# Other step counts for convolution and pooling chains in a hybrid pooling and convolution block

## The chip, the cores and the metric

The kernel runs on one core of one Trainium2 chip. The metric is the device time in microseconds (us), the median of several runs. The engines are TensorE (PE, with its weight loads as PEld), VectorE (DVE), ScalarE (ACT), GpSimd (POOL) and SyncE (SP), which issues most of the DMAs.

## The reference

One layer (DEPTH 1), 2048 frames, model width 1024, float32. What is computed:

```python
h = rmsnorm(x, norm_mix_pre[l])
proj = h @ w_in[l]
u_pool, u_glu, g_a, g_b = jnp.split(proj, [512, 1536, 2560], axis=-1)
branch_a = pool_mixer(u_pool, pool_w[l], pool_scale[l], w_pool_out[l])
branch_b = conformer_conv(u_glu, conv_w[l], conv_b[l], conv_ln_g[l], conv_ln_b[l], w_conv_out[l])
merged = jax.nn.sigmoid(g_a) * branch_a + jax.nn.sigmoid(g_b) * branch_b
x = x + rmsnorm(merged @ w_o[l], norm_mix_post[l])
h = rmsnorm(x, norm_mlp_pre[l])
f = jnp.square(jax.nn.relu(h @ w_up[l])) @ w_down[l]
x = x + rmsnorm(f, norm_mlp_post[l])
```

`pool_mixer` takes trailing means over 2, 4, 8 and 16 frames minus the frame itself, a linear map for each of the 4 groups of 128 channels, a scale and a projection. `conformer_conv` is a gated unit, a causal depthwise convolution of 31 taps over 512 channels, a LayerNorm, a swish and a projection.

## The kernel before, in words

The frames are worked on in two blocks of 1024 (`b` 0 and 1). Channels lie on the 128 partitions, frames along the free axis. The large matrix products use a scheme of seven products instead of eight for two-by-two blocks; such a group of seven is an `Octet` (products 1, 2, 6, 5, 7, 3, 4 in this order, the first two octets of a run mixed by `START`). Each operand is a high and a low part of reduced precision, made by `split` and `split_w` (ScalarE rounds the high part at L195 or L202, VectorE subtracts at L119). So one product is 24 matmuls of 128x128 by 128x512 (L240). The low parts of the weights (`wl`) are computed for block 0, stored in `kept`, and loaded again for block 1.

The order of the main line is: for block 0 the octets `glu` (two), `pool` (one), `ga` (two), `gb` (two), then the product `A` (the pooling branch, `branch_a`, eight tiles); for block 1 `pool`, `glu`, `ga`, `gb`; then block 0's `B` (`merge`, eight tiles) and `wo` (`out_proj`, eight tiles of two products each), block 1's `A`, block 0's `up` (eight octets), block 1's `B`, `wo` and `up`, and `down` for both blocks. Products are counted here from 0 in this order: ga begins at 21, gb at 35, A at 49, block 1's pool at 57, its ga at 78, its gb at 92, B at 106, wo at 114, A at 130, up at 138.

Beside the main line run the chains of the change. `conv_steps` does the convolution on VectorE, 31 taps for each of four channel groups, one step a tap (L756 for the first, L760 for the others); the group's sum is added (`sm`), and the row stored to DRAM (`yd`). `pool_steps` does the window sums (L116, L869), a split, six matmuls on TensorE (`mix`), an evacuation (L881 on ScalarE, L882 on VectorE) and a store to `mxd`, from where `A` loads it. `norm_steps` is the LayerNorm: matmuls L790 and L791 for the mean, subtractions of the mean from rows loaded again, L438 for the sum of squares, the root (small instructions of L461 to L493), L505 to spread it over the partitions, then scale, swish and a store to `zd`, from where `B` loads it.

A chain is a Python generator in a `Lane`. After each product, `bg()` calls each lane, which adds its `rate` to a credit and takes so many steps; a step that yields a number ends the turn and skips products. The instructions of these steps are put behind the product's mark (`behind`), and a scheduler then orders each engine by priority. `tc.high_priority(offset=...)` moves instructions forward in this order. On the chip each engine works in its order, SP's queue of DMAs too, so what stands behind a waiting instruction waits as well. The `tr` tiles (nine buffers), `wl` (three), `wr` (four) and the PSUM tiles for products (three) are shared by main line and chains; the accumulator `y` of the convolution has one buffer.

`tail` is the lane of block 0's convolution and pooling; what is left of it goes on in block 1 as the lane at L1202, behind which the norm of block 0 follows. `pooling()` (L1204) adds, after block 1's `pool` octet, a lane for its pooling and one for its convolution, `conv1`, which waits for the other two. `conv1` goes on in B (rate 0.5), `wo` (the rate of L1223) and `up` (1.2, then 2.8), with block 1's norm behind it.

Of the kernel before, what the change touches and what calls it, by code (L numbers as in the profile page):

```python
# [65 lines left out]
def block_kernel(  # L66
# [132 lines left out]
    def split_w(src, n=TB, low=None):  # L199
        hi = mk(p_wh, "wh", F32R)  # L200
        lo = mk(p_wl, "wl", F32R)
        nc.scalar.copy(hi[:, :n], src[:, :n])  # L202
        if low is None:
            sub(lo[:, :n], src[:, :n], f32(hi[:, :n]))
        else:
            load(f32(lo), low)
        return hi, lo
# [3 lines left out]
    def load_w(src, key):  # L211
        with tc.high_priority(offset=ahead[0]):
            raw = mk(p_wr, "wr")
            load(raw, src)
            known = kept.get((key, "low"))
            w = split_w(raw, low=known)
        if known is None:
            kept[key, "low"] = dram("kept")
            later.append((kept[key, "low"], f32(w[1])))
        return w  # L220

    kept, later, due = {}, [], []
# [45 lines left out]
    def weight_parts(src, key, b, keep, raw):  # L268


        s = {}

        def get(q):
            if q not in raw:
                raw[q] = mk(p_wr, "wr")
                load(raw[q], src[q])
            return raw[q]

        def minus(a, b, op=sub):
            o = mk(p_ws, "ws")  # L280
            op(o, a, b)
            return o

        def source(i):
            if i in (1, 2, 4):
                return get({1: 0, 2: 1, 4: 3}[i])
            if (key, i, "sum") in kept and b:
                if ("s", i) not in raw:
                    raw["s", i] = mk(p_wr, "wr")
                    load(raw["s", i], kept[key, i, "sum"])  # L290
                return raw["s", i]
            if i == 7:
                return minus(get(0), get(2))
            if i in (5, 6) and 1 not in s:
                s[1] = minus(get(2), get(3), add)
            if i == 6:
                s[2] = minus(s[1], get(0))
                return s[2]
            if i == 5:
                return s[1]  # L300
            return minus(get(1), s[2])

        def save(i, what, tile):
            kept[key, i, what] = dram("kept")
            later.append((kept[key, i, what], f32(tile)))

        def part(i):
            with tc.high_priority(offset=ahead[0]):
                for q in {1: (0,), 2: (1,), 4: (3,), 7: (0, 2), 5: (2, 3), 6: (2, 3, 0), 3: (1,)}[i]:
                    if (key, i, "sum") not in kept or not b:  # L310
                        get(q)
                if (key, i, "sum") in kept and b:
                    source(i)
            with tc.high_priority(offset=40):
                t = source(i)
                w = split_w(t, low=kept[key, i, "low"] if keep and b else None)
            if keep and not b:
                save(i, "low", w[1])
                if keep == "sums" and i not in (1, 2, 4):
                    save(i, "sum", t)  # L320
            return w

        return part
# [451 lines left out]
    def norm_steps(b, lag):  # L775

        sh, sl = split(sums[b], *TR)
        yield 3
        mu = mk(p_ss, "r", F32, (P, W))[:, :TB]
        y = {}  # L780

        def prefetch(c):
            y[c] = tr()
            load(y[c], yd[b, c, 0])

        prefetch(0)
        for t in (0, 1):
            s = slice(t * T, (t + 1) * T)
            rb = mk(ps_rb, "rb", F32, (P, T))
            nc.tensor.matmul(rb, ones, sh[:, s], start=True, stop=False)  # L790
            nc.tensor.matmul(rb, ones, sl[:, s], start=False, stop=True)  # L791
            nc.scalar.activation(mu[:, s], rb, AF.Copy, scale=1.0 / CW)
        yield 1
        ss = mk(p_ss, "sm")
        for c in range(CC):
            if c + 1 < CC:
                prefetch(c + 1)
            sub(y[c], y[c], mu)
            load(yd[b, c, 0], y[c])
            sq = ss if c == 0 else tr()  # L800
            nc.scalar.activation(sq, y[c], AF.Square)
            if c % 2:
                yield 1
            if c:
                add(ss, ss, sq)
        yield lag
        r = mk(p_ss, "r", F32, (P, W))[:, :TB]
        halves = [ss[:, t * T : (t + 1) * T] for t in (0, 1)]

        def got(t, rb):  # L810
            nc.scalar.copy(r[:, t * T : (t + 1) * T], rb)

        yield from inv_rms_steps(halves, inv_c, TR, lag, got)
        prefetch(0)
        yield 1
        sg, hl = {}, {}
        for c in range(CC + 2):
            if c < CC:
                if c + 1 < CC:
                    prefetch(c + 1)  # L820
                mul(y[c], y[c], r)
                sg[c] = tr()
                nc.scalar.activation(
                    sg[c], y[c], AF.Sigmoid, scale=col(C_LG + c), bias=col(C_LB + c)
                )
                nc.scalar.activation(
                    y[c], y[c], AF.Identity, scale=col(C_LG + c), bias=col(C_LB + c)
                )
            if 0 < c <= CC:
                mul(y[c - 1], y[c - 1], sg[c - 1])  # L830
                hl[c - 1] = split(y[c - 1], *TR)
            if c > 1:
                for i, part in enumerate(hl[c - 2]):
                    load(zd[b, c - 2, i], f32(part))
            yield 1
# [9 lines left out]
    def pool_steps(b, alone):  # L845

        def get(g):
            s, u = window(W), tr()
            load(s, ud[g][:, b * TB : b * TB + W])
            load(u, ud[g][:, HALO + b * TB : HALO + b * TB + TB])  # L850
            return s, u

        s, u = get(0)
        yield 1
        for g in range(CC):
            w, m = WINDOWS[g], 1
            while m < w:
                lo = HALO - (w - 2 * m)
                s2 = window(W) if alone or m in (2, 8) else mk(p_ss, "r", F32, (P, W))
                add(s2[:, lo:], s[:, lo:], s[:, lo - m : W - m])  # L860
                s, m = s2, 2 * m
                yield
            if b == 0:
                mul(
                    s[:, HALO : HALO + w],
                    s[:, HALO : HALO + w],
                    cst[:, C_CNT + g * HALO : C_CNT + g * HALO + w],
                )
            nc.vector.scalar_tensor_tensor(  # L869
                u, s[:, HALO:], 1.0 / w, u, op0=ALU.mult, op1=ALU.subtract  # L870
            )
            hl = split(u, *TR)
            if g + 1 < CC:
                s, u = get(g + 1)
            yield 3
            ps = psum("mix")
            for t in (0, 1):
                h = slice(t * T, (t + 1) * T)
                matmuls(ps[:, h], pw, g, [tuple(p[:, h] for p in hl)], main=False)
            hi, lo = tr(F32R), tr(F32R)  # L880
            nc.scalar.activation(hi, ps, AF.Copy, scale=col(C_PSC + g))  # L881
            nc.vector.scalar_tensor_tensor(  # L882
                lo, ps, col(C_PSC + g), f32(hi), op0=ALU.mult, op1=ALU.subtract
            )
            yield
            load(mxd[b, g, 0], f32(hi))
            load(mxd[b, g, 1], f32(lo))
            yield
# [238 lines left out]
    lanes = []  # L1127
# [25 lines left out]
    tail = Lane(1.9, conv_steps(0, (0,)))  # L1153
# [18 lines left out]
    def more():  # L1172
        pool_weight()
        tail.gens.append(chain_of(pool_steps(0, True), conv_steps(0, (1, 2, 3), False)))
        tail.rate = 2.2

    pi = pool_in(0, parts)[0]
    run(
# [6 lines left out]
    rest = tail.gens  # L1185
# [6 lines left out]
    def marked(gen, k):  # L1192
        yield from gen
        done.add(k)
# [4 lines left out]
        yield from gen  # L1199

    rest = [marked(chain_of(*rest), "conv")]
    lanes += [Lane(3.8, *rest, marked(norm_steps(0, 1), "norm"))]  # L1202

    def pooling():  # L1204
        lanes.append(Lane(2, marked(pool_steps(1, False), "pool")))
        lanes.append(Lane(2.0, behind_all(conv_steps(1, (0, 1, 2, 3)), "conv", "pool")))


# [8 lines left out]
    conv1 = lanes.pop()  # L1217
# [2 lines left out]
    lanes.append(conv1)  # L1220
    merged = merge(0, bg)
    fetched = []
    conv1.rate = 2  # L1223
    parts = Parts(lambda ops: token_parts(ops, lambda c, t: parts.raw(c, t), *BIG, TR))
    chain = out_proj(
        0, merged, ((0,), (1,)), bg, parts.some, lambda: fetched.extend(fetch_spread(mxd, 1))
# [301 lines left out]
    for n, (s, i, b) in enumerate(jobs):  # L1528
# [8 lines left out]
        if s == LAST or b == 0:  # L1537
            w = [part(i, o) for o in (0, 1)]
# [80 lines left out]
```

## Time and profile before

| | |
|---|---|
| median of 3 runs | 2405.51 us (2405.14 to 2408.62) |
| profiled execution | 2413.18 us, its span 2411.4 us |
| mean granted TensorE clock in it | 0.965 |
| TensorE matmul, busy | 2234.3 us, 93% of the span |
| weight load, busy | 1824.6 us, 76% |
| VectorE, busy | 1688.1 us, 70% |
| ScalarE, busy | 1036.1 us, 43% |
| DMA | 566.98 MB, mean 235 GB/s |

The profile is one execution, taken by the hardware profiler. A line of a profile names the source line, the engine, the operation and the tiles as output<-inputs. In brackets at the end of an instruction stands how long the engine was idle before it and what ended that. Busy matmuls overlap, so the pace of TensorE is read from their number in a stretch (x714 in 160 us) and not from the busy time. A row of stages gives the stretch in us from the span's start, its length, busy time and count for PE, PEld, DVE, ACT and POOL, the granted clock as a share, the DMA engines' share and GB/s.

### The profile page before, as it was taken

Reading aid. Unit: us, or ns where it says so; the run is one execution under the profiler, and the core shown is the slowest. Engines: PE = TensorE matmul, PEld = TensorE weight load, DVE = VectorE, ACT = ScalarE, POOL = GpSimd, SP = SyncE. Lnnn points to the kernel's source line nnn. Section 1 sums busy time; section 2 is a strip of 40 time slices with the busy share of each in tenths; the row PEclk is TensorE's granted clock in tenths of the full one; section 3 lists DMA queues with packets and bytes.
Section 4 is the critical chain, followed back from the end, with each engine's and each line's share of the span. In section 5 each row is a group of like instructions: output and inputs, shape, how many; then the busy total and the mean of one; then the engine's idle time right before and its main releaser. Section 6 shows DMA issues by size and latency. Waiting matters only on the chain.

```text
span 2411.4 us, 25045 instructions
## 1 busy us (share of the span) xinstructions
PE 2234.3 (93%) x9600; PEld 1824.6 (76%) x9600; DVE 1688.1 (70%) x1672; ACT 1036.1 (43%) x1077; POOL 1.0 (0%) x10
## 2 busy tenths in 40 slices
PE   6999988897989989999989988999999999999984
PEld 5788877686778877787868866888788887788763
DVE  5897757897668549898644496777644656696776
ACT  5434442333532425444543564555544322223542
POOL 0000000000000000000000000000000000000000
PEclk9999999998999989999999989999999999999996
DMA  4678997676897774335496655687755445447873
GB/s 169 245 263 294 345 349 250 231 246 232 293 352 283 254 290 158 131 128 181 160 360 251 221 198 210 229 301 261 296 203 192 164 162 201 178 148 250 291 285 156
DMA packets 158951, 566.98 MB, mean 235 GB/s; under 512 B 18672, under 2 KB 18800, under 8 KB 158832
## 3 DMA queue, kind: packets, MB, share of 16 engines
q1 hardware_dynamic: 146448, 520.30, 59.9%
q10 hardware_dynamic: 12384, 45.09, 4.8%
q8 instruction: 75, 1.23, 0.2%
q14 instruction: 44, 0.36, 0.0%
HBM read 378.06 MB, written 187.27 MB: 234 GB/s over the span
## 4 chain that ended last, share of the span: by engine, by line
PE 72%; DVE 15%; DMA 6%; issue 4%; ACT 3%; SPq 0%; DVEq 0%; ACTq 0%
PE down L240 23%; PE up L240 17%; PE wo L240 7%; PE gb L240 5%; DVE y L760 4%; PE ga L240 4%; PE B L240 4%; PE glu L240 4%; PE A L240 4%; PE pool L240 3%; DVE tr L119 2%; DVE tr L116 2%; DMA tr<-yd 2%; DMA wr<-w_in 1%; DVE wl L119 1%
## 5 line engine op out<-in xcount | busy, mean ns | idle before, releaser
L240 PE MATMUL up<-big,wh 128*128 128x512 f32 x1792 | 493.7, 397 | 42.7 <-ACT tr L390 21.4
L240 PEld LDWEIGHTS up<-big,wh 128*128 128x128 f32 x1792 | 341.8, 192 | 121.9 <-ACT tr L390 24.0
L202 ACT CAST wh<-wr 128x1024 fp32r<-128x1024 f32 x176 | 185.0, 1051 | 467.4 <-issue 80.5
L240 PE MATMUL down<-tr,wh 128*128 128x512 f32 x896 | 353.6, 395 | 13.0 <-DVE tr L119 13.0
L240 PE MATMUL down<-fo,wh 128*128 128x512 f32 x896 | 352.9, 394 | 9.6 <-ACT fo L1383 9.5
L760 DVE SCALAR_TENSOR_TENSOR y<-v,cst,y 128x1024 f32<-128x1024 f32 x240 | 307.1, 1280 | 3.2
L240 PE MATMUL up<-big,wl 128*128 128x512 f32 x896 | 280.8, 395 | 0.0
L240 PE MATMUL down<-fo,wl 128*128 128x512 f32 x896 | 278.9, 393 | 0.0
L202 ACT CAST wh<-ws 128x1024 fp32r<-128x1024 f32 x124 | 130.3, 1052 | 257.9 <-PE up L240 97.0
L240 PEld LDWEIGHTS down<-tr,wh 128*128 128x128 f32 x896 | 170.0, 190 | 53.1 <-DVE tr L119 18.0
L240 PEld LDWEIGHTS down<-fo,wh 128*128 128x128 f32 x896 | 170.2, 190 | 48.6 <-ACT fo L1383 13.3
L240 PEld LDWEIGHTS up<-big,wl 128*128 128x128 f32 x896 | 171.6, 192 | 36.3
L240 PEld LDWEIGHTS down<-fo,wl 128*128 128x128 f32 x896 | 170.0, 190 | 35.3
L1383 ACT CAST fo<-tr 128x1024 fp32r<-128x1024 f32 x102 | 107.0, 1050 | 188.0 <-DMA tr<-fd 128.3
L116 DVE TENSOR_TENSOR big<-big,down 128x1024 f32<-128x1024 f32 x88 | 106.9, 1218 | 110.4 <-PE down L240 105.9
L119 DVE TENSOR_TENSOR wl<-ws,wh 128x1024 fp32r<-128x1024 f32 x116 | 141.5, 1220 | 58.3 <-ACT wh L202 57.9
L119 DVE TENSOR_TENSOR tr<-tr,fo 128x1024 fp32r<-128x1024 f32 x102 | 124.6, 1221 | 72.9 <-ACT fo L1383 72.7
L119 DVE TENSOR_TENSOR wl<-wr,wh 128x1024 fp32r<-128x1024 f32 x103 | 125.5, 1218 | 46.5 <-ACT wh L202 45.9
L240 PE MATMUL glu<-big,wh 128*128 128x512 f32 x448 | 127.3, 405 | 21.5 <-DVE big L119 9.2
L240 PE MATMUL ga<-big,wh 128*128 128x512 f32 x448 | 123.3, 398 | 6.2 <-DVE tr L116 5.9
L240 PE MATMUL wo<-big,wh 128*128 128x512 f32 x512 | 127.1, 390 | 0.2 <-DVE big L119 0.2
L116 DVE TENSOR_TENSOR tr<-tr,tr 128x1024 f32<-128x1024 f32 x65 | 79.4, 1221 | 66.6 <-ACT tr L536 57.9
(151 smaller groups left out, 3147.9 us busy)
## 6 DMA issues: line engine op xcount, KB each, us to landing
tr<-fd SPq DMA_DIRECT2D x116, 512.0 KB, 5.3
wl<-kept SPq DMA_DIRECT2D x81, 512.0 KB, 4.0
wr<-w_up SPq DMA_DIRECT2D x68, 512.0 KB, 4.3
wr<-w_down SPq DMA_DIRECT2D x66, 512.0 KB, 4.3
kept<-wl SPq DMA_DIRECT2D x65, 512.0 KB, 5.3
fd<-tr ACTq DMA_DIRECT2D x54, 512.0 KB, 3.5
wr<-w_in SPq DMA_DIRECT2D x53, 512.0 KB, 5.6
fd<-tr SPq DMA_DIRECT2D x50, 512.0 KB, 3.5
```

The lines of the kernel that those rows point to most:

```text
L116: return nc.vector.tensor_tensor(o, a, b, op=ALU.add)
L119: return nc.vector.tensor_tensor(o, a, b, op=ALU.subtract)
L202: nc.scalar.copy(hi[:, :n], src[:, :n])
L240: i = nc.tensor.matmul(ps, w[wp][:, (at + k) * P : (at + k + 1) * P], rhs[k][xp], start=start and n == 0, stop=stop and n == len(order) - ...
L760: nc.vector.scalar_tensor_tensor(acc, v[:, k : k + TB], wk, acc, op0=ALU.mult, op1=ALU.add)
L1383: nc.scalar.copy(hi, t)
```

## The change

Four rates change, and two scopes of priority are written in another way.

```diff
@@ load_w
-            w = split_w(raw, low=known)
+            w = split_w(raw) if known is None else None
+        if w is None:
+            with tc.high_priority(offset=260):
+                w = split_w(raw, low=known)
@@ weight_parts, part
-                w = split_w(t, low=kept[key, i, "low"] if keep and b else None)
+                if not (keep and b):
+                    w = split_w(t)
+            if keep and b:
+                with tc.high_priority(offset=40):
+                    w = split_w(t, low=kept[key, i, "low"])
@@ more
-        tail.rate = 2.2
+        tail.rate = 3
@@ 
-    lanes += [Lane(3.8, *rest, marked(norm_steps(0, 1), "norm"))]
+    lanes += [Lane(3.2, *rest, marked(norm_steps(0, 1), "norm"))]
@@ pooling
-        lanes.append(Lane(2, marked(pool_steps(1, False), "pool")))
+        lanes.append(Lane(1.7, marked(pool_steps(1, False), "pool")))
@@ 
     merged = merge(0, bg)
     fetched = []
-    conv1.rate = 2
+    conv1.rate = 6
```

The number of instructions is the same; their order differs. In the two orders the convolution taps stand in these stretches of VectorE:

| stretch of VectorE's order | taps before | taps after |
|---|---|---|
| up to the end of block 0's pool octet | 15 | 15 |
| block 0's ga and gb, first two reads of A | 16 | 34 |
| from there to the read of block 1's 30th product | 93 | 75 |
| the rest of block 1's ga and gb, B | 36 | 31 |
| from B's last read to the first read of block 1's A (wo) | 17 | 47 |
| block 0's up | 71 | 46 |

| on TensorE, the place ahead of product | before | after |
|---|---|---|
| block 0's four mixes | 32, 37, 42, 48 | 30, 34, 38, 43 |
| block 1's four mixes | 72, 77, 82, 88 | 73, 78, 84, 91 |
| first matmul of block 0's norm (L790) | 87 | 87 |
| first matmul of block 1's norm (L790) | 174 | 165 |

## The prediction

> **What bounds the kernel now.** I began with the busy times of the page, then the stages cut at the borders of the matrix products, and last the waits inside the stages that lose time.
>
> ```profile
> PE 2234.3 (93%) x9600; PEld 1824.6 (76%) x9600; DVE 1688.1 (70%) x1672; ACT 1036.1 (43%) x1077; POOL 1.0 (0%) x10
> ...
> 160.00:320.00 160.00, 160.00 (x714) 132.43 (x713) 124.25 (x138) 69.04 (x70) 0.00 (x0) 1.00 0.84 310
> ...
> 386.00:590.00 204.00, 178.72 (x736) 143.50 (x736) 180.28 (x151) 65.50 (x65) 0.00 (x0) 0.93 0.68 237
> 590.00:720.00 130.00, 117.67 (x484) 96.25 (x485) 80.07 (x84) 57.95 (x60) 0.00 (x0) 0.93 0.85 306
> ...
> 852.00:912.00 60.00, 52.91 (x205) 42.14 (x204) 32.33 (x42) 15.36 (x19) 0.00 (x0) 0.86 0.78 290
> ...
> 1004.00:1116.00 112.00, 112.00 (x496) 92.72 (x494) 111.41 (x96) 51.38 (x50) 0.00 (x0) 1.00 0.33 124
> ...
> 1204.00:1249.00 45.00, 35.74 (x148) 29.10 (x147) 23.45 (x21) 25.43 (x25) 0.00 (x0) 0.89 0.95 349
> ```
>
> A row gives the length of a stage, then busy time and instruction count for PE, PEld, DVE and ACT, then the granted clock. In a stretch without a gap TensorE does 714 matmuls in 160 us, 4.46 per us, so one product of 24 matmuls takes 5.4 us. At that pace 386:590 needs 736 / 4.46 = 165 us and took 204: 39 us are lost. The same sum gives 21.5 us lost in 590:720, 14 in 852:912 and 12 in 1204:1249. From 1004 to 1116 VectorE is busy all the time and TensorE still loses nothing: a full VectorE is no loss as long as nobody waits for it. The change touches only chains on VectorE, so its worth is read from the stages where TensorE waits for them.
>
> ```profile
> PE rb L790 <- ACT tr L195: 12.3, 1, 12.3
> PE pool L240 <- DMA wl<-kept: 5.4, 1, 5.4
> PE glu L240 <- DVE tr L116: 5.4, 1, 5.4
> ```
>
> These are TensorE's longest waits in 386:590. The first is the mean of the convolution: its operand is split on ScalarE, after the last convolution tap of block 0. Two of the three hang on the depth of VectorE's queue, the one in the middle is a load of weights.
>
> **The change, part by part.** The two rewritten priority scopes cost nothing: with them alone, the build has the same instructions, buffers and waits in the same order on every engine. What is left is four rates. The counts below are those of the two orders, as tabled above.
>
> *Rate 2.2 to 3: block 0's gates and the start of A.* Pooling must be done before the product A.
>
> ```profile
> 320.00:340.00 20.00, 13.90 (x51) 10.65 (x50) 4.87 (x4) 5.11 (x6) 0.00 (x0) 0.83 0.97 373
> ...
> 323.51 1.29 DVE tr L882
> ...
> 324.82 5.25 DMA mxd<-tr
> ...
> 330.12 5.75 DMA big<-mxd
> ...
> 334.68 0.80 PE L240 MATMUL A<-big,wh 128*128 128x512 f32 x1 [5.66 <-DMA big<-mxd]
> ...
> 336.93 2.76 PE L240 MATMUL A<-big,wh 128*128 128x512 f32 x6
> ...
> 340.98 1.52 PE L240 MATMUL A<-big,wh 128*128 128x512 f32 x6
> ```
>
> The last pooling result is made, stored and loaded again in 12.3 us (323.51 to 335.87) while TensorE stands. In the slice 320:340 it does 51 matmuls, worth 11.4 us: 8.6 us lost. The last mix moves from ahead of product 48 to ahead of product 43, five products or 27 us earlier, so the 12.3 us are covered: gain 8.6, nothing else of that load being late. The row also shows that a stop costs more than its idle time: six matmuls take 2.76 us right behind it and 1.52 us later. The Trainium skill, "TensorE: Matmul & The Clock Gate", Part 1, says that an idle window of about 3.4 us halves the clock until a busy window has passed; the trace agrees (2.76 against 1.52 us). By that rule the stop would cost its 5.66 us and half a window, 7.4; the sum takes the slice's 8.6.
>
> The price: 18 convolution taps move into this stage and the first two A products.
>
> ```profile
> L760 DVE SCALAR_TENSOR_TENSOR y<-v,cst,y 128x1024 f32<-128x1024 f32 x240 | 307.1, 1280 | 3.2
> ...
> L119 DVE TENSOR_TENSOR wl<-ws,wh 128x1024 fp32r<-128x1024 f32 x116 | 141.5, 1220 | 58.3 <-ACT wh L202 57.9
> ...
> 290.00:320.00 30.00, 30.00 (x134) 24.79 (x133) 16.46 (x16) 11.72 (x13) 0.00 (x0) 1.00 0.98 355
> ```
>
> 18 x 1.28 = 23 us of VectorE. In 160:320 it has 160 - 124 = 36 us to spare, 13.5 of them after 290, where most taps go, and pooling work of about six instructions leaves that place. Behind the taps on VectorE stand the low halves of weights (wl) and the gates' sums; whoever is late there stops TensorE. I take 3 us of loss, between 0 (the spare time holds all) and 8 (a third of the 23 us shows).
>
> *Rates 3.8 to 3.2 and 2 to 1.7: block 1's pool, glu and ga.* Up to the 30th product of block 1, where norm and pooling meet, VectorE has 75 taps instead of 93 and three pooling instructions fewer: 18 x 1.28 + 3 x 1.22 = 26.7 us less, from 180.3 to 153.6 us. TensorE needs 165. So VectorE stops being the longer side. If its own idle time stays (204 - 180 = 24 us), the stage takes 154 + 24 = 178 us; TensorE alone, with the load of weights kept (5.4 us and a slow clock behind), about 173 (5.4 x 8.6 / 5.66 = 8). The gain is at most 27; at least some 8, if the 12.3 us of L790 shrink to a third and all other waits stay, since they come from the order of the queue. I take 20: the sum for VectorE gives 26, and I leave 6 to waits that the order makes. L790 stands ahead of product 87 in both orders, and I expect it to lose most of its 12.3 us.
>
> *The rest of block 1's gates.* Pooling ends later (mix ahead of product 91, before 88), beside the norm steps.
>
> ```profile
> 603.11 1.23 DVE L119 TENSOR_TENSOR tr<-tr,r 128x1024 f32<-128x1024 f32 x1 [8.22 <-DMA tr<-yd]
> ...
> 620.52 2.93 PE L240 MATMUL ga<-big,wh 128*128 128x512 f32 x6 [5.88 <-DVE tr L116]
> ```
>
> VectorE waits 8.22 us for a stored convolution row to come back, and the gate's sum behind it holds TensorE for 5.88 us. The loads stand among the same neighbours in both orders, so this stays. Five taps fewer lie behind it, but pooling's tiles now share the nine `tr` buffers with the norm. I take a gain of 2, between -6 (that wait once more) and +6 (it is gone).
>
> *Rate 2 to 6: the output projection.* From its first tile to the first read of A, VectorE has 47 taps instead of 17: 30 x 1.28 = 38.4 us more.
>
> ```profile
> 763.00:798.00 35.00, 35.00 (x156) 29.00 (x155) 34.02 (x29) 14.17 (x17) 0.00 (x0) 1.00 0.57 180
> 798.00:858.00 60.00, 57.63 (x251) 46.69 (x250) 23.78 (x34) 30.60 (x39) 0.00 (x0) 0.98 0.79 280
> 858.00:879.00 21.00, 17.31 (x63) 13.62 (x62) 0.34 (x2) 1.05 (x1) 0.00 (x0) 0.82 0.72 274
> ...
> 797.75 1.23 DVE L116 TENSOR_TENSOR tr<-tr,tr 128x1024 f32<-128x1024 f32 x1
> 808.63 1.23 DVE L116 TENSOR_TENSOR tr<-tr,tr 128x1024 f32<-128x1024 f32 x1 [9.65 <-ACT tr L536]
> 809.89 0.69 DVE L116 TENSOR_TENSOR tr<-tr 128x512 f32<-128x512 f32 x1
> 818.51 0.16 DVE L461 TENSOR_SCALAR sa<-rb 128x4 f32<-128x4 f32 x1 [7.93 <-PE rb L438]
> ...
> 878.75 1.22 DVE L122 TENSOR_TENSOR tr<-A,tr 128x1024 f32<-128x1024 f32 x1 [20.66 <-DMA tr<-sad]
> ```
>
> VectorE's first 35 us are full and keep nearly the same taps (17; 18 of the 47 now); the others fall into 798:858, with 36 us free, and before 878.75, where it waits 20.66 us for a gate. Laid out one after the other: the square sum of 797.75 ends about 2.5 us later (a tap, a convolution's sum), 801.5; 8 taps bring it to 812; the sums of 808.63 and 809.89 with a tap between them end at 815, not 810.6; 4 taps and a sum later, at 821.5, the root begins that began at 818.51. Its input, the sum, is taken by TensorE's L438, which VectorE waited 7.93 us for, so 4.4 us later is early enough. 14 taps among the adds behind it (18 us) fill waits there and end the stretch some 8 us later than now, near 866, still ahead of 878.75. ScalarE's gains (L571) wait for some of these adds, with reads of PSUM behind them. I take 2 us of loss, between 0 and 18 (all 14 taps among the adds show). The loss in 852:912 has another cause, the loads of A, and stays.
>
> *The end of block 0's up products.* With 46 taps left instead of 71, the second norm starts ahead of product 165, not 174, and is over before the last two octets, which have extra stores.
>
> ```profile
> PE up L240 <- ACT tr L390: 9.3, 1, 9.3
> ...
> 1203.11 3.73 SPq L125 DMA_DIRECT2D fd<-tr  x3
> 1206.93 0.44 SPq L125 DMA_DIRECT2D tr<-yd  x1
> ...
> 1213.32 1.22 DVE L122 TENSOR_TENSOR tr<-tr,r 128x1024 f32<-128x1024 f32 x1 [3.30 <-DMA tr<-yd]
> ```
>
> The norm's last load stands behind those stores on SP's queue; VectorE waits for it, ScalarE for VectorE, TensorE for ScalarE: 9.3 us, 12 with the slow clock. I take 9.5 gained, between 2 (the norm meets a like stop earlier) and 12. That the taps of 1004:1116 go gains nothing: TensorE lost nothing there.
>
> **The sum**: 8.6 - 3 + 20 + 2 - 2 + 9.5 = 35.1 us. The profiled execution took 2413.2 us (span 2411.4 and 1.8 around it), so it would take 2378. It was 7.7 us above the median of the runs, 2405.5; 35.1 off that is 2370.4.
>
> **The rivals.** *Order, not depth*: the waits of 386:590 come from where the instructions stand and not from how many there are. For it: the three longest waits there make 23 of the 39 us, one of them is a load of weights, and the rest are short pieces. Against: VectorE was busy 88% of that stage. Then 3 of the 20 us are won, 18 in all: 2387. *All of it*: each gain at its upper bound and no loss, 8.6 + 27 + 6 + 12 = 53.6: 2352.
>
> *The projection pays* (slower): six taps a tile hold VectorE's adds back, ScalarE's gains wait for them ahead of its reads of PSUM, and TensorE stops in each tile of the second half. The price is 38.4 us of taps, and 1.52 times that where the clock falls (8.6 us lost for 5.66 of waiting at A's start): 58 us, against the 2 in the sum: 2370 + 56 = 2426. It decides once over 37 us show, that is, if hardly any of the 58 us that VectorE stands idle from 763 to 879 can be used. For it: in-order adds with ScalarE behind. Against: its longest idle times end at TensorE and a load, not at its own work.
>
> *Nothing moves*: all of it is shifted within the slack. The Trainium skill, "Perfetto Trace Analysis", Identifying the Most-Contended Engine, says to improve the engine with the highest occupancy; here that is TensorE (93%) and the change takes no work from it, so by that rule alone the time stays 2405.5. The trace speaks against it: 5.66 us of waiting for pooling at A and 12.3 at L790 are idle TensorE. That the rates do nothing at all is excluded by the orders.
>
> **How the numbers follow.** Forecast 0.62, order 0.18, all of it 0.07, the projection 0.10, nothing moves 0.03. About 0.2%, 5 us, is what a measurement of this kernel can tell from no change. Faster is 0.62 + 0.18 + 0.07 = 0.87, of which 0.01 may end within 5 us: 0.86; same 0.04; slower 0.10. The bounds of the terms reach from 54 us won to 13 lost if all fall together; the forecast's own range is 2354 to 2388. With the order rival and the full gain inside, and the projection left out, the range is 2348 to 2400.
>
> **What would show it.** Right: no wait on mxd at the first A product of block 0; L790 below 4 us; VectorE under 95% of a stage from pool to ga that is some 20 us shorter; no stop near the end of the first up, and a norm over before it; roots in the projection less than 5 us later against their product. Wrong: new waits of TensorE for wl or for L505 in the projection, a mix that waits beside the norm, or waits as long as before in block 1's glu with fewer taps in front of them.

## The result and the profile after

The kernel with the change took 2364.76 us in the median of 4 runs (2361.49 to 2370.55). The kernel before, on the same chip, took 2405.32 us (2402.55 to 2408.62, 4 runs). The ratio is 0.9833, with a 95% interval of 0.981 to 0.9857: 1.7% or some 41 us faster. In a second set of runs (**e0_again**) it took 2370.28 us beside 2411.61, a ratio of 0.9827 [0.9805, 0.9848]. The profiled execution took 2370.55 us, its span is 2368.8 us against 2411.4 before.

The first fence holds the page's busy times, the next one the stages, cut where a product's first matmul runs: block 0's ga and gb (164:325), its A (325:368), then block 1's pool and glu, ga and gb, block 0's B and `wo`, block 1's A, and block 0's `up`. The change shifts all lines of the file after its first edits by 3 to 7: L240, L390, L438, L505, L760 and L790 are now L243, L397, L445, L512, L767 and L797.

```profile
PE 2223.5 (94%) x9600; PEld 1818.9 (77%) x9600; DVE 1690.4 (71%) x1672; ACT 1037.7 (44%) x1077; POOL 1.0 (0%) x10
```

```profile
164.00:244.00 80.00, 80.00 (x358) 66.17 (x357) 70.83 (x77) 35.76 (x36) 0.00 (x0) 1.00 0.80 290
244.00:325.00 81.00, 81.00 (x362) 67.03 (x361) 68.56 (x75) 34.57 (x36) 0.00 (x0) 1.00 0.94 344
325.00:368.00 43.00, 43.00 (x192) 35.60 (x190) 31.76 (x27) 20.80 (x27) 0.00 (x0) 1.00 1.00 380
368.00:511.00 143.00, 127.32 (x518) 102.04 (x517) 115.23 (x97) 48.83 (x49) 0.00 (x0) 0.93 0.70 239
511.00:603.00 92.00, 87.03 (x371) 70.87 (x370) 71.11 (x77) 37.81 (x39) 0.00 (x0) 0.94 0.80 279
603.00:688.00 85.00, 80.00 (x340) 65.16 (x340) 55.40 (x47) 42.40 (x42) 0.00 (x0) 0.96 0.95 350
688.00:735.00 47.00, 44.13 (x196) 36.21 (x195) 35.10 (x30) 12.51 (x13) 0.00 (x0) 1.00 0.92 339
735.00:824.00 89.00, 89.00 (x398) 73.76 (x397) 80.81 (x83) 38.99 (x48) 0.00 (x0) 1.00 0.72 244
824.00:884.00 60.00, 51.67 (x202) 41.41 (x201) 44.01 (x52) 17.13 (x22) 0.00 (x0) 0.86 0.80 303
884.00:1204.00 320.00, 311.81 (x1370) 256.95 (x1369) 243.42 (x224) 172.97 (x172) 0.00 (x0) 0.99 0.49 178
```

VectorE and ScalarE are busy as long as before, to 2.3 us. Of the 42.6 us that the span lost, 31.8 were idle time of TensorE; the other 10.8 us are a lower busy time for the same 9600 matmuls. A of block 0 and the projection (735:824) run without a gap, the projection with VectorE at 80.8 of 89 us. Block 1's pool to ga still loses, at a granted clock of 0.93, with VectorE at 79% (115.23 + 71.11 of 235 us). Block 1's A (824:884) loses as much as before.

TensorE's waits that answer to those of the prediction, in the whole of the span:

```profile
PE pool L243 <- DMA wl<-kept: 7.4, 1, 7.4
...
PE up L243 <- ACT tr L397: 6.9, 3, 4.7
...
PE gb L243 <- DMA wl<-kept: 5.0, 2, 4.2
PE A L243 <- DMA tr<-mxd: 4.4, 2, 2.3
PE ga L243 <- ACT tr L736: 4.2, 1, 4.2
```

The norm's mean (L790, 12.3 us) is no longer among them, and the waits of `up` for L390 (now L397) are shorter: the 9.3 us one is gone, and the 4.7 left is in block 1's `up`. Two smaller ones, inside B of block 0 and A of block 1:

```profile
PE B L243 <- DMA big<-zd: 2.9, 1, 2.9
```

```profile
PE A L243 <- DVE tr L122: 3.9, 1, 3.9
```

The table compares stages of the profiled executions, each from the first matmul of a product to the first of the next, in us. "Again" is e0_again; the other columns are the experiments below. The prediction drew one border in another place: its stage "pool, glu and ga" ends ahead of product 87, inside ga.

| stage | before | changed | again | e1 | e2 | e3 | e4 | e6 | e7 | e8 | e9 | e10 | e12 | e13 |
|---|---|---|---|---|---|---|---|---|---|---|---|---|---|---|
| ga and gb, block 0 | 161.0 | 161.0 | 161.0 | 161.0 | 161.0 | 161.0 | 161.0 | 161.0 | 161.0 | 161.0 | 161.0 | 161.0 | 161.0 | 161.7 |
| A, block 0 | 52.2 | 43.5 | 43.5 | 44.9 | 52.2 | 53.0 | 53.7 | 43.5 | 53.4 | 43.5 | 43.5 | 43.5 | 43.5 | 43.5 |
| pool, glu, block 1 | 145.4 | 142.9 | 143.8 | 149.2 | 143.6 | 148.0 | 144.7 | 146.3 | 144.2 | 136.2 | 143.3 | 140.8 | 147.1 | 145.9 |
| ga, block 1 | 107.8 | 91.7 | 93.0 | 94.4 | 80.6 | 107.0 | 94.5 | 95.3 | 80.0 | 84.5 | 90.1 | 90.3 | 108.0 | 108.2 |
| gb, block 1 | 87.3 | 85.2 | 84.1 | 85.1 | 92.8 | 88.2 | 87.0 | 85.6 | 94.6 | 85.9 | 83.8 | 84.5 | 76.2 | 76.2 |
| B, block 0 | 43.5 | 46.7 | 48.9 | 43.5 | 54.6 | 43.5 | 43.5 | 43.5 | 54.0 | 45.0 | 45.1 | 44.8 | 43.5 | 43.5 |
| wo, block 0 | 88.5 | 88.5 | 88.5 | 88.5 | 88.5 | 88.5 | 88.5 | 88.5 | 88.5 | 88.5 | 88.5 | 88.5 | 88.5 | 88.5 |
| A, block 1 | 59.8 | 60.5 | 61.8 | 55.6 | 58.5 | 52.3 | 54.4 | 53.1 | 59.8 | 59.2 | 61.7 | 51.0 | 53.1 | 52.3 |
| up, block 0 | 337.1 | 320.0 | 319.8 | 339.4 | 333.3 | 319.8 | 340.2 | 319.6 | 319.8 | 320.2 | 331.5 | 320.1 | 320.1 | 321.4 |
| B, block 1 | 43.5 | 43.5 | 43.5 | 43.5 | 59.5 | 43.5 | 43.5 | 43.5 | 43.5 | 43.5 | 43.5 | 43.5 | 43.5 | 43.5 |

From before to changed: A -8.7, pool and glu -2.5, ga -16.1, gb -2.1, B +3.2, A of block 1 +0.7, `up` -17.1. That is -42.6 us, the difference of the two spans. What stands ahead of and behind these stages cancels: the start is 1.9 us earlier, the `up` of block 1 3.8 us shorter, and the rest (`down`) 5.8 us longer (691.3 against 685.5).

### The profile page after: what moved, and what is told of

Read it like the earlier page. It is cut to its first block, busy times and chain, and to the rows that moved or that the text cites. A ratio compares the mean times of both kernels' runs of the same rounds, so it can differ in the third digit from the quotient of the medians.

```text
span 2368.8 us, 25052 instructions
## 1 busy us (share of the span) xinstructions
PE 2223.5 (94%) x9600; PEld 1818.9 (77%) x9600; DVE 1690.4 (71%) x1672; ACT 1037.7 (44%) x1077; POOL 1.0 (0%) x10
## 4 chain that ended last, share of the span: by engine, by line
PE 79%; DVE 10%; DMA 6%; issue 2%; ACT 2%; SPq 0%; DVEq 0%; ACTq 0%
PE down L243 24%; PE up L243 23%; PE wo L243 7%; PE ga L243 5%; PE gb L243 5%; PE glu L243 4%; PE A L243 4%; PE B L243 4%; PE pool L243 2%; DVE tr L119 2%; DMA tr<-fd 1%; DVE tr L116 1%; DVE y L767 1%; DVE big L116 1%; DMA wr<-w_in 1%
## 5 line engine op out<-in xcount | busy, mean ns | idle before, releaser
L243 PE MATMUL up<-big,wh 128*128 128x512 f32 x1792 | 489.9, 395 | 28.5 <-ACT big L195 10.3
L243 PEld LDWEIGHTS up<-big,wh 128*128 128x128 f32 x1792 | 339.7, 190 | 105.8 <-ACT big L195 12.4
L243 PE MATMUL down<-tr,wh 128*128 128x512 f32 x896 | 354.9, 396 | 12.2 <-DVE tr L119 12.2
L243 PE MATMUL down<-fo,wh 128*128 128x512 f32 x896 | 354.1, 395 | 11.9 <-ACT fo L1390 11.9
L767 DVE SCALAR_TENSOR_TENSOR y<-v,cst,y 128x1024 f32<-128x1024 f32 x240 | 307.6, 1282 | 3.6
L243 PE MATMUL down<-fo,wl 128*128 128x512 f32 x896 | 280.6, 395 | 0.0
L243 PE MATMUL up<-big,wl 128*128 128x512 f32 x896 | 279.2, 393 | 0.0
L243 PEld LDWEIGHTS down<-tr,wh 128*128 128x128 f32 x896 | 170.8, 191 | 53.3 <-DVE tr L119 17.9
L243 PEld LDWEIGHTS down<-fo,wh 128*128 128x128 f32 x896 | 171.0, 191 | 50.3 <-ACT fo L1390 14.6
L243 PEld LDWEIGHTS down<-fo,wl 128*128 128x128 f32 x896 | 171.4, 191 | 35.7
L243 PEld LDWEIGHTS up<-big,wl 128*128 128x128 f32 x896 | 170.4, 190 | 35.8
L1390 ACT CAST fo<-tr 128x1024 fp32r<-128x1024 f32 x102 | 107.0, 1050 | 188.0 <-DMA tr<-fd 120.2
L119 DVE TENSOR_TENSOR wl<-wr,wh 128x1024 fp32r<-128x1024 f32 x103 | 125.6, 1220 | 43.5 <-ACT wh L202 41.0
L243 PE MATMUL glu<-big,wh 128*128 128x512 f32 x448 | 125.2, 399 | 18.8 <-DVE big L119 10.0
L243 PE MATMUL wo<-big,wh 128*128 128x512 f32 x512 | 127.1, 390 | 0.2 <-DVE big L119 0.2
L243 PE MATMUL ga<-big,wh 128*128 128x512 f32 x448 | 123.0, 397 | 4.2 <-ACT tr L736 4.2
L243 PE MATMUL gb<-big,wh 128*128 128x512 f32 x448 | 121.6, 394 | 0.0
```

The lines of the kernel that those rows point to most:

```text
L119: return nc.vector.tensor_tensor(o, a, b, op=ALU.subtract)
L243: i = nc.tensor.matmul(ps, w[wp][:, (at + k) * P : (at + k + 1) * P], rhs[k][xp], start=start and n == 0, stop=stop and n == len(order) - ...
L767: nc.vector.scalar_tensor_tensor(acc, v[:, k : k + TB], wk, acc, op0=ALU.mult, op1=ALU.add)
L1390: nc.scalar.copy(hi, t)
```

## Experiments

> The changed kernel itself once more, so that the next ones can be compared with it on the same chip: 2365 us, 40 below before.

That was 2370.28 us, as told above; in the stages of the table its profile agrees with the first to 2.2 us. Two theories were open. By *depth*, what counts is how much of VectorE's own work stands ahead of a product, whatever its order. By *order*, what counts is where a few instructions stand: the norm's mean, its stores and loads, the gates' loads.

### One rate alone

**e1_tail3**: the first rate alone.

```diff
-        tail.rate = 2.2
+        tail.rate = 3
```

> Only the first rate changes (2.2 to 3). The last mix of block 0 stands ahead of product 43 and block 1 starts with 18 taps fewer, while its own lanes keep 3.8 and 2. Depth theory: the stop at the first A goes (-8.6 us) and the stretch from block 1's pool to the start of its gb loses most of 18 x 1.28 = 23 us, some 16: in all -25 us, about 2380. Order theory (waits there come from where instructions stand): -8.6 and about -3, about 2393.

Measured: 2383.22 us, ratio 0.9897 [0.9877, 0.9917]. Block 0's A loses its stop, and block 1 from pool to gb's start falls from 253.2 to 243.6 us: 9.6 us, between the 16 of depth and the 3 of order. All of it is won behind product 87; up to there the stretch takes 213.8 us, before 211.0, with 18 taps fewer in it. The time is near the forecast all the same, with A of block 1, among others, 4.2 us shorter. The wait for the norm's mean falls, in the waits of block 1:

```profile
PE pool L240 <- DMA wl<-kept: 7.5, 1, 7.5
PE glu L240 <- DVE tr L116: 5.5, 1, 5.5
...
PE rb L790 <- ACT tr L195: 3.2, 1, 3.2
```

The glu's wait is as it was and the load's 2.1 us longer, 12.3 us has become 3.2: the 18 taps that went ahead are seen in the wait that hangs on the last tap. The mean now stands ahead of product 82 and not 87, so this run alone doesn't tell the taps from the place.

**e2_lanes**: the two lower rates alone.

```diff
-    lanes += [Lane(3.8, *rest, marked(norm_steps(0, 1), "norm"))]
+    lanes += [Lane(3.2, *rest, marked(norm_steps(0, 1), "norm"))]
...
-        lanes.append(Lane(2, marked(pool_steps(1, False), "pool")))
+        lanes.append(Lane(1.7, marked(pool_steps(1, False), "pool")))
```

> Only the two lanes of block 1 change (3.8 to 3.2, 2 to 1.7). Up to the 30th product of block 1 VectorE has 80 taps instead of 93, but the taps are only put off: the norm of block 0 starts ahead of product 93, not 87. Depth theory: the stretch up to ga loses some 12 us, and part of it comes back in gb and B, where the norm now ends close to its reader: -8 us, about 2397, no stop at L790. Order theory: within 3 us of before. The stop at the first A (8.6 us) stays in either.

Measured: 2409.73 us, ratio 1.0005 [0.9993, 1.0017], no change, and no 8 us. ga of block 1 is 27.2 us shorter. Then gb takes 5.5 more, B of block 0 11.1 and B of block 1 16.0. (Up to product 87 alone it is 195.6 us, before 211.0.) The waits inside the B of block 1 show what was put off:

```profile
PE B L240 <- DMA big<-zd: 11.9, 3, 9.6
```

`zd` is what the norm stores. Fewer taps a product means a shorter queue now and a later norm, and B reads the norm's result: in block 0 the last store of `zd` is issued 7 us ahead of B, before it was 35. The lower rates by themselves take nothing away, they defer it.

**e3_wo6**: only the projection's rate.

```diff
-    conv1.rate = 2
+    conv1.rate = 6
```

> Only the rate in the output projection changes (2 to 6). The norm of block 1 starts ahead of product 163 instead of 174. If the prediction's term was right, block 0's up is 9.5 us shorter; if the whole norm got cheaper by its earlier place, 17 us, as in the changed kernel. The projection itself: 0 to 2 us longer, 38 to 58 us if the rival that it pays is right. Forecast 2390, with 2396 for the smaller gain.

Measured: 2386.27 us, ratio 0.9904 [0.9885, 0.9923]. `up` is 17.3 us shorter, `wo` unchanged, A of block 1 7.5 us shorter. The 11.4 us wait for the mean is still there, as it must be:

```profile
PE rb L790 <- ACT tr L195: 11.4, 1, 11.4
```

### Depth measured by itself

**e4_skip18** is the kernel before, **e8_after_skip18** the changed one, each with the same edit: 18 taps of block 0 are left out, while their steps are still counted, so that the order of all others stays.

```diff
+                if b == 0 and c in (2, 3) and k % 3 == 2 and k < 28:
+                    yield
+                    continue
```

> The kernel before, but 18 of the convolution's 124 taps of block 0 are left out (every third one of channel groups 2 and 3); the steps are still counted, so nothing else moves. It takes 23 us of VectorE's work out of the stretch from block 1's pool to its ga. Depth theory: this stretch gets some 16 to 20 us shorter and L790 waits under 4 us; the stop at the first A stays: about 2387. Order theory: the waits stay, at most 5 us, about 2401.

> The changed kernel with 18 taps of block 0's convolution left out (every third of channel groups 2 and 3, the steps still counted): 23 us less work on VectorE in the stretch from block 1's pool to its ga. If VectorE's depth still bounds that stretch after the change, it loses another 10 us or more: 2355. If the change has brought it to where order and loads bound it, within 4 us of the changed kernel.

Measured: 2394.42 us, ratio 0.9938 [0.9915, 0.9961], and 2353.24 us, ratio 0.9763 [0.9745, 0.9781]. Block 1's stretch from pool to gb, one row for each of before, changed, e4 and e8:

```profile
379.00:632.00 253.00, 216.32 (x884) 174.16 (x884) 207.15 (x179) 85.52 (x86) 0.00 (x0) 0.91 0.70 241
```

```profile
368.00:603.00 235.00, 214.35 (x887) 172.90 (x886) 186.34 (x172) 86.64 (x87) 0.00 (x0) 0.93 0.74 255
```

```profile
381.00:620.00 239.00, 215.25 (x885) 173.69 (x884) 183.88 (x168) 85.51 (x86) 0.00 (x0) 0.93 0.72 253
```

```profile
368.00:589.00 221.00, 206.20 (x888) 167.54 (x887) 161.18 (x139) 86.06 (x87) 0.00 (x0) 0.97 0.78 268
```

All four do the same 885 or so matmuls, worth 198 us. Taking the 18 taps out (VectorE's busy time falls by 23 and 25 us) makes the stretch 14 us shorter in both kernels, though VectorE was busy only 82% and 79% of it. In e4 that is less than the 16 to 20 us forecast, and the wait for the mean is gone, as depth had it. So depth counts in this stretch before and after, at some 0.6 us for each us of taps. What makes the rest of its loss these two runs don't show.

### Together, and in another place

**e7_no_tail3** has the lower rates and the projection's 6, without the first rate; **e6_no_lanes** has the first rate's 3 and the projection's 6, without the lower rates.

```diff
 e7_no_tail3, against the changed kernel
-        tail.rate = 3
+        tail.rate = 2.2
 e6_no_lanes, against the changed kernel
-    lanes += [Lane(3.2, *rest, marked(norm_steps(0, 1), "norm"))]
+    lanes += [Lane(3.8, *rest, marked(norm_steps(0, 1), "norm"))]
...
-        lanes.append(Lane(1.7, marked(pool_steps(1, False), "pool")))
+        lanes.append(Lane(2, marked(pool_steps(1, False), "pool")))
```

> The first and the last rate as changed (3 and 6), the two lanes of block 1 as before (3.8 and 2). If the changes add up by stage, it is 25 + 23 us under before, some 2359, and the 6 us under the changed kernel come from B, which no longer waits for zd (3 us), and from the mean of the norm, which starts ahead of product 82, not 87. If the lower rates of the lanes are what makes block 1's glu and ga shorter, as the prediction had it for 20 us, it is slower than the changed kernel: 2372 or more.

> The kernel before with the lanes' rates 3.2 and 1.7 and conv1 at 6, without the first rate's 3. Theory 'the first rate carries block 1': the stretch from block 1's pool to B's end gains nothing, as with the lower rates alone, and only the 17 us of block 0's up remain: about 17 to 19 us under the kernel before, some 2390. Rival, the prediction's own account (the lower rates on VectorE give block 1 most of its gain): 17 us of up and 15 or more of block 1 together, 2377 or less.

Measured: e6 2364.95 us, ratio 0.9813 [0.979, 0.9835]; e7 2379.94 us, ratio 0.9875 [0.9856, 0.9894]. From block 1's pool to the end of block 0's B, before took 384.0 us (145.4 + 107.8 + 87.3 + 43.5), e1 372.2, e2 371.6, e7 372.8, e6 370.7, the changed kernel 366.5. Either edit alone wins 11 to 13 us there and both win 17.5, so their gains overlap. In e7 the lower rates keep what they lost again in e2, since the projection's rate makes block 1's norm early: its B takes 43.5 us instead of 59.5. So e7, 29.7 us under the kernel before, comes out between the two forecasts, nearer to the prediction's.

The lower rates win about 4 us here over e6, their loss in B counted, and e6 is still not slower than the changed kernel: it takes 53.1 instead of 60.5 us in A of block 1. Its time lies between its two forecasts (2359, and 2372 or more). The intervals overlap, so e6 is not shown faster; but of the four rates the two lower ones are not shown to be worth anything in the end.

**e9_norm_late**: the changed kernel with block 1's norm held back by nine products, to where it was before.

```diff
-    conv1.gens.append(norm_steps(1, 2))
+    def later_norm():
+        for _ in range(9):
+            yield 1
+        yield from norm_steps(1, 2)
+
+    conv1.gens.append(later_norm())
```

> The changed kernel with the norm of block 1 held back by nine products, so that it starts ahead of product 174 as in the kernel before; the taps stay where the change has put them (46 in block 0's up). If the place of the norm made the 17 us in block 0's up: they come back, 2380 to 2383, with a stop near the end of up behind a load of yd. If the smaller number of taps made them: up stays at 320 us, 2365.

Measured: 2378.11 us, ratio 0.9865 [0.9844, 0.9886]. The median is 7.8 us above e0_again's, and the two intervals just overlap, so the stages decide. `up` takes 331.5 us, 11.5 more than in the changed kernel, though the same taps were done in the projection. The wait near its end is back, and the last stretch of `up` loses 11 us (of its 43 us the 141 matmuls are worth 31.6):

```profile
PE up L243 <- ACT tr L397: 8.6, 1, 8.6
```

```profile
1172.00:1215.00 43.00, 34.39 (x141) 27.92 (x141) 21.98 (x20) 24.10 (x25) 0.00 (x0) 0.88 0.95 359
```

So some two thirds of the gain in `up` is the norm's place, not the number of taps left.

### The gates of block 1's A

In the changed kernel, VectorE stands idle for 11.99 us in A of block 1, waiting for a gate from DRAM. Its row on VectorE, and SyncE's queue:

```profile
834.13 3.92 DVE L767 SCALAR_TENSOR_TENSOR y<-v,cst,y 128x1024 f32<-128x1024 f32 x3
850.03 1.23 DVE L122 TENSOR_TENSOR tr<-A,tr 128x1024 f32<-128x1024 f32 x1 [11.99 <-DMA tr<-sad]
```

```profile
827.62 1.49 SPq L125 DMA_DIRECT2D big<-xt  x2
842.00 0.33 SPq L125 DMA_DIRECT2D wl<-kept  x1
842.37 0.91 SPq L125 DMA_DIRECT2D big<-xt  x2
843.32 1.10 SPq L125 DMA_DIRECT2D tr<-sad  x2
```

The queue issues nothing from 829 to 842: a load of weights waits there for its buffer, 11.3 us of that for a matmul of A, and the gates (`sad`) stand behind it. **e10_gate_first** is the changed kernel with these loads ahead.

```diff
-            load(sg, sad[(b, *k)])
+            if b:
+                with tc.high_priority(offset=40):
+                    load(sg, sad[(b, *k)])
+            else:
+                load(sg, sad[(b, *k)])
```

> The changed kernel, with block 1's four gate loads (sad) given priority over the weight loads that follow them in the list, so that the SyncE queue takes tr<-sad ahead of the wl<-kept that waits for TensorE. Theory 'the queue's order': block 1's first projection waits for its gates because they stand behind that load; then A of block 1 falls from 60.5 us to about 53, PE A <- DVE tr from 3.9 us to under 1, and the time is about 7 us under the changed kernel: 2360. Rival 'VectorE is late': the gates wait for the taps ahead of them on VectorE, whatever the queue does; then A of block 1 stays at 60 to 62 us and the time at 2365 to 2370.

Measured: 2357.15 us (5 runs), ratio 0.9776 [0.9756, 0.9797]. Its queue and its stage:

```profile
819.07 1.30 SPq L125 DMA_DIRECT2D tr<-sad  x2
...
835.65 0.32 SPq L125 DMA_DIRECT2D wl<-kept  x1
```

```profile
818.00:869.00 51.00, 47.02 (x203) 38.22 (x202) 45.28 (x53) 17.96 (x22) 0.00 (x0) 0.97 0.90 349
```

The weight load still waits, from 823 to 835, but two gates are ahead of it. A of block 1 takes 51.0 us instead of 60.5, 9.5 us less where some 7 were forecast; `up` and B behind it are unchanged, and TensorE's 3.9 us wait for VectorE is gone. The median is 7.6 us under the changed kernel's first one; by the ratios it is 0.5 to 0.6%, some 13 us. The profile is of the fastest of its runs, so the rest of its shorter span is not put down to the edit. Its interval lies under those of both runs of the changed kernel: it beats both kernels.

**e12_tail35** and **e13_both** take the first rate on to 3.5, with the lower rates as before; e13 has the gate loads ahead too.

```diff
 against e6_no_lanes; e13_both also has the edit of e10_gate_first
-        tail.rate = 3
+        tail.rate = 3.5
```

> The changed kernel with the two lanes' rates as before (3.8 and 2) and the first rate at 3.5 in place of 3: 55 taps instead of 49 stand ahead of block 1. Theory 'depth': six taps fewer, of about 0.81 us each by the 18 that gave 14.5 us, are owed behind block 1's pool; the stretch from block 1's pool to its gb loses about 5 us against the 241.6 of the kernel with rates 3 and 6 alone, and the time is about 2360. Rival 'the first stretch is full': VectorE in block 0's ga and gb has no room for more, the stretch of 161 us for the two or block 0's A grows by as much as is saved later, and the time is 2365 to 2370.

> The two edits of the other kernels together: first rate 3.5, the two lanes' rates as before, conv1 at 6, and block 1's gate loads ahead of the weight load. If the queue's order and the depth are both right and the lanes' rates alone moved the gates, A of block 1 is 53 us already without the edit of the loads, so the two don't add: about 2358 to 2360. If the gate loads matter on their own, 2353 to 2355.

Measured: 2370.08 us, ratio 0.9836 [0.9816, 0.9855], and 2366.1 us, ratio 0.9817 [0.9799, 0.9836]. Neither forecast of e12 names the place: block 0 has room (161.0 and 43.5 us), and yet block 1 from pool to gb takes 255.1 us, where e6 takes 241.6. gb then takes 9.4 us less than there. A wait of 6.9 us for a load of `wl` and one stop in ga stand out. In time, across three engines of e12:

```profile
531.17 1.05 ACT L202 CAST wh<-ws 128x1024 fp32r<-128x1024 f32 x1 [8.11 <-DVE ws L119]
...
533.39 1.22 DVE L116 TENSOR_TENSOR sm<-sm,y 128x1024 f32<-128x1024 f32 x1
...
534.64 1.04 ACT L195 CAST tr<-sm 128x1024 fp32r<-128x1024 f32 x1 [2.43 <-DVE sm L116]
535.59 1.01 ACT L397 COPY tr<-ga 128x1024 f32<-128x1024 f32 x1
...
536.65 2.93 PE L243 MATMUL ga<-big,wh 128*128 128x512 f32 x6 [9.07 <-ACT tr L397]
```

The copy that empties a tile of ga in PSUM (535.59) stands on ScalarE behind a rounding of weights, which waits 8.11 us for VectorE, and behind the norm's split (L195), which waits 2.43 us more; TensorE waits 9.07 us for the copy. In e6 the first copy of ga stands ahead of both. Block 0's last convolution sum comes six taps earlier in e12, which may have moved the split. Fewer taps ahead, and a worse place: here order seems to have beaten depth. That the place alone does it is read from these rows and was not tested. e13 differs from e12 by less than their intervals, which fits that A of block 1 is at 53.1 us without its edit; both are slower than forecast, with this stop in ga.

## Why the prediction was right, and where it was not

The forecast of 2370.4 us is 5.6 above the median. The direction held, and in the main the mechanism: TensorE stopped less behind chains on VectorE. The sum of 35.1 us was 42.6 in the profile, and its terms came out unevenly. That the whole fits so well is in part luck, since terms were wrong in opposite ways.

- *A's start: 8.6 us.* It was 8.7. A of block 0 starts on time at a granted clock of 1.00, with no wait on `mxd` at its first product; e1 has 7.3 of it by the first rate alone. In the prediction's words TensorE stands for the 12.3 us of the store and load; it worked on for most of that and stood for 5.66, which is what the sum rests on.
- *The price in block 0's ga and gb: -3.* It was 0. VectorE's busy time in the two rose from 122.1 to 139.4 us of 161, and nobody waited.
- *Block 1's pool, glu and ga: 20.* In the prediction's own stage, up to product 87, it was 9.7 (211.0 to 201.3 us from block 1's first product), half of the term and near its lower bound of 8; from the matmul at 386, where its row begins, it was 11.7. Before, and then after, with the stage behind it:

```profile
379.00:590.00 211.00, 180.30 (x743) 144.47 (x742) 186.45 (x157) 70.34 (x70) 0.00 (x0) 0.92 0.68 237
```

```profile
368.00:570.00 202.00, 182.07 (x747) 146.70 (x746) 164.67 (x138) 70.47 (x70) 0.00 (x0) 0.93 0.70 242
570.00:688.00 118.00, 112.28 (x481) 91.36 (x480) 77.06 (x82) 58.57 (x59) 0.00 (x0) 0.96 0.95 346
```

The step that failed is "if its own idle time stays": VectorE lost 22 us of work and its idle time grew from 25 to 37 us. It is at 82% of the stage, under the 95% of the forecast, but the stage isn't some 20 us shorter. The wait for the mean (12.3 us) went, but the load of weights took 7.4 us instead of 5.4, and a wait of ga for ScalarE of 4.2 us is new, at 560.78. The rival "order, not depth" had 3 us here. e4 and e8 speak against it, with 13.5 and 13.8 us for 18 taps in this stage; e1 speaks for it, with 18 taps fewer there, 10 us less of VectorE's work and no gain. So both count. The gain was filed under the lower rates, and here they do carry it (e2 195.6 us, e1 213.8), but they give it back behind: alone they end at a ratio of 1.0005.

- *The rest of the gates: 2.* It was 10.9 (129.5 to 118.6 us), over the upper bound of 6: 8.9 in the rest of ga and 2.1 in gb. The wait of 5.88 us that "stays" went. That it would stay, since the loads have the same neighbours, is the step that failed; which of the changed places made it go is open. The 20 and the 2 make 22 together and measured 20.6, by luck.
- *Missing from the sum: B of block 0.* B waits 2.9 us for `zd` and takes 3.2 us more. The norm doesn't end late: its last store of `zd` is issued at 650.9, 37 us ahead of B, before it was 35. What is late is the last load of it, on SyncE's queue:

```profile
685.45 0.33 SPq L125 DMA_DIRECT2D wr<-w_o  x1
685.83 0.44 SPq L125 DMA_DIRECT2D big<-zd  x1
```

It is issued 2.5 us ahead of B (688.30) behind a load of weights, and takes 7.7 us; before, the last one was issued 7 us ahead. What moved it there is open. In e6, with the lanes' rates as before, B takes 43.5 us. In e2, where the norm does end late, this term is 11.1 us, and 16 in the other block.

- *The projection: -2.* It was 0. Laid out one after the other, the taps were to end near 866 on the clock of before; after, the last ends at 838.05, which is 103.1 us behind the first product of `wo` and would be 866.2 there. The root starts 56.1 us behind that product (791.11, less 734.98), before it was 55.4: under 5 us later, as forecast. The slower rival falls: all 30 taps went into idle VectorE and nobody stopped.
- *The end of `up`: 9.5.* It was 17.1, mis-sized the other way. The wait of 9.3 us at its end and the slow clock behind it were worth about 11.5 (e9), near the upper bound of 12. Most of the other 5.6 stood in a place for which the prediction had no term: where the norm of before begins beside `up`, 177 matmuls were done in 44 us in which 196 fit, 4.3 us lost:

```profile
1116.00:1160.00 44.00, 39.18 (x177) 31.30 (x176) 31.52 (x41) 25.44 (x27) 0.00 (x0) 1.00 0.65 235
```

The changed kernel begins its norm at 1042, inside this row, and e9 at 1090, inside the next:

```profile
976.00:1088.00 112.00, 112.00 (x504) 93.04 (x503) 94.42 (x88) 58.31 (x58) 0.00 (x0) 1.00 0.44 160
```

```profile
1088.00:1132.00 44.00, 44.00 (x203) 36.49 (x202) 30.53 (x42) 24.36 (x26) 0.00 (x0) 1.00 0.57 209
```

Neither loses anything there (504 in 112 us and 203 in 44 are 4.5 and 4.6 a us). "The norm meets a like stop earlier", the lower bound, did not happen. As e9 begins it at the place of before, the smaller number of taps left (46 against 71) is the likely cause that this stop went; no run changed that number alone.

- *The loss in A of block 1 stays.* It did (60.5 against 59.8). The prediction called it the loads of A; e10 shows that 9.5 of its 17 us over block 0's A (60.5 against 43.5) are gate loads behind a weight load. The rest is open: waits for `mxd`, 4.0 us there, and the clock behind them are still there.

*Nothing moves* gave 2405.5 and fell: the idle time of TensorE that went, with the slow clock behind it, was worth 1.7%. Beside it stood the Trainium skill, "Perfetto Trace Analysis", Identifying the Most-Contended Engine, which says to optimize the engine with the highest occupancy first. That the time stays when no work leaves that engine was the prediction's inference, and the page doesn't say it. For TensorE it prefers the busy share of the weight loads to that of the matmuls; by this share too (76%, VectorE 70%) it is TensorE, and most of what went was time in which TensorE waited.

The stages after show the clock much as the prediction read it: 0.86 to 0.96 is granted in block 1's pool to gb and its A, where waits of 3.9 to 7.4 us remain, and 1.00 in A of block 0, where the wait went. B of block 0, with a wait of 2.9 us, has 1.00 too.

## What to carry to other kernels

A chain that runs beside the main line has two readers: whoever stands behind its steps in the queue, and whoever reads its result. Lowering its rate pays the first and charges the second, so a rate is worth setting only with the result's due time in hand; taking steps earlier, into stretches where the engine is idle and nobody waits, pays both. And where a load seems late, look first at what stands ahead of it in its queue: here two gate loads moved past one waiting load shortened their stage by 9.5 us.

## What the runs showed of the hardware

The price of a stop is no fixed multiple of its idle time. The prediction had 1.52 (8.6 us for 5.66). One wait of 2.9 us in B took 3.2 us at a granted clock of 1.00, and the 8.6 us wait in e9 took 11.4 at 0.88. In block 1's A, waits of 8.3 us (4.4 for `mxd`, 3.9 for VectorE) go with 60.5 us where block 0's A takes 43.5, at a clock of 0.86: twice as much. In e10 4.0 us of waiting for `mxd` are left there, with 51.0 us and a clock of 0.97.

VectorE can lengthen a stretch in which it is busy only 79% of the time: e8 took 25 us of its work out of 235 us and won 14.
